# Three rows of score maxima taken in the first stage, output rows prepared in four stages, and other distances in the first stage's chains

## The chip, the cores and the metric

One core of a Trainium2 chip runs the whole kernel. The metric is the device time of one execution in microseconds (us), as the median of several runs. TensorE (PE) does the matmuls, VectorE (DVE), ScalarE (ACT) and GpSimd (POOL) the element work; every transfer here is issued by SyncE (SP). Each engine takes its instructions strictly in the order in which the program holds them.

## What is computed

The reference is one layer of a hybrid encoder block on x of 4096 rows and 1024 columns:

```python
u = rms_norm(h, pre_norm_gain[layer])
proj = jnp.einsum('bsd,de->bse', u, w_in[layer])
fq, fk, fv, fz, ff, rq, rk, rv, rz = jnp.split(proj, split_points, axis=-1)
fox = forgetting_attention(q, k, v, ff + forget_bias)   # 8 heads of 64: causal softmax of
...                                # q.k/8 + c[t] - c[s], c = cumsum(log_sigmoid(f_logit))
fox = fox.reshape(b, s, FOX_WIDTH) * jax.nn.silu(fz)
ret = retention(rq, rk, rv)        # 4 heads of 128: rotation, decayed chunks, group norm
ret = ret.reshape(b, s, RET_WIDTH) * jax.nn.silu(rz)
mixed = jnp.concatenate([fox, ret], axis=-1)
out = jnp.einsum('bse,ed->bsd', mixed, w_out[layer])
h = h + rms_norm(out, post_norm_gain[layer])
```

(The heads' reshapes are left out.) Everything is float32; the kernel gets that accuracy from fp16 pairs (high and low part), with three matmul passes for one product.

## The kernel before

**Stages.** `phase_f0` is the first stage. It computes the input projection of attention heads 0 to 3 (q, k, v, gate z and the forget logits of all 8 heads) for 8 blocks `b` of 512 rows. A block has four units `unit_T` (j = 0 to 3: q, q, k, k) and four units `unit_N` (t = 0 to 3: v and z of 128 rows each). A unit has 8 k-steps of 3 matmuls (6 half-wide ones in `unit_N`). Then `attention()` runs 64 items (one head and one block of 512 queries each). An item of query block qb has 4(qb+1) steps; one step is a pair of score matmuls, two exponentials on ACT (`pf` L1140, `ph` L1141), a subtraction on POOL (`pl` L312) and, six steps later, the product with v. Between attention steps, fillers are issued as long as a credit lasts: the projection of heads 4 to 7 (`fill_f1`), retention in two groups (`fill_r`), and the output projection (`fill_o`). What of `fill_o` is left after the attention runs alone.

**What sets the order.** The program is scheduled by hand. Everything that follows a matmul is a chain, a Python generator in the list `chains`. `tick()` advances every chain by one `yield`; it is called once per k-step of the first stage (`f0_tick`), per attention step and per filler step. So a chain's distance from its source is counted in ticks, and where an instruction stands in its engine's order is fixed when the program is built. A DVE instruction whose input is late holds up all DVE instructions behind it. All PSUM results rotate through 8 banks (`PS()`); a matmul into a bank waits until the bank's last reader is done.

**Weights of the next group.** `scales(1)` reads the 16 tiles of the second projection group (`w_raw`, one transfer `rw` each, issued on SP), takes each one's maximum on DVE (`w_max`, L229) three steps of `SAGE` = 4 ticks after the place of its issue, and then forms the scale. It is started with block 5. `f1.load()`, started with block 6, reads the same tiles again and splits them: ACT writes the high part (L220), DVE the low part (L150). `rw` shares one pool of 12 buffers (`b2`) with the tiles `s2` and `pf`.

**Forget gates.** After each block `forget_block` turns the forget logits into log-sigmoid values (15 small DVE operations, one per tick, and one exponential on ACT), and `VAGE` = 5 ticks later multiplies them on PE with a triangular matrix (`csb`, 128x128, 4 matmuls). These matmuls stand inside the next block's stream, and the same is so for `c_parts`, which splits the cumulated sums into three fp16 parts, one operation per tick, and writes them out.

**Maxima of the score rows.** An item needs, before its first step, a bound on each query's scores. `max_tile()` forms one 128x512 tile of scores on PE, adds a mask on a diagonal tile and reduces it on DVE (L1006). With its last tile an item's `max_row` follows: reduce (L1018), 9 ticks, a transpose on PE (L1024), `mr` on ACT (L1026), two DVE operations, a transfer out (`MR`) and two back into the item's `xq`. `until(("m", n))` lets ticks pass until the last of these is issued. Items 0, 1 and 2 need 4, 8 and 12 tiles. In the last block, items 0 and 1 are done in one burst each, after units t = 0 and t = 1; item 2's tiles go at most two per attention step.

**Evacuation.** `evac_qk` (ACT L401, then DVE L150) empties a `unit_T` bank, `evac_vz` (ACT L425 and L427, then DVE, among it the forget logits at L429) the two banks of a `unit_N`. `rope_evac` empties a q or k bank of retention with ACT (L761) and, `ACTAGE`+1 = 3 ticks later, starts four DVE operations on the copy; the transposes of retention (L818) need the result.

**Output rows.** `prep(n)` prepares 128 rows: a maximum over the row (DVE L1185), small DVE operations, a scaling of the whole tile on ACT (L1188), then two halves of four transposes on PE (L1196) with a copy on ACT and a subtraction on DVE. The first part is issued in one piece. While attention runs, all of `prep` is issued filler step after filler step; in the tail it stands between the matmuls of the row before. `o_final` does the post-norm with a power on POOL.

## Time and profile before

| what | us |
|---|---|
| median of 3 runs | 3123.46 (3123.4 to 3123.75) |
| the profiled execution | 3122.3 |
| its span, first to last instruction | 3120.5 |
| PE busy in the span | 3018.6 (97%) |
| DVE, ACT, POOL busy | 2069.3, 1869.0, 1359.8 |
| first stage, 0 to 428.28 | PE idle in blocks 5 to 7: 3.42, 4.83, 5.39 |
| attention to the first output row, 428.28 to 2677.96 | PE busy 2197.55 of 2249.68 |
| start of the output rows, 2677.96 to 2698.99 | PE busy 11.20 of 21.03 |
| rest, 2698.99 to 3120.5 | PE busy 405.35 of 421.51 |

Every engine but PE has slack over the whole span, so an idle stretch counts where it is PE's. PE's matmuls also run at two clocks: a granted clock (PEclk) of 1.00 or of 0.50, and a stretch at 0.50 holds half the work. The rows behind this are given further down, in numbered groups.

### The profile page before, as it was taken

How to read it: one execution, taken by the hardware profiler on the slowest of the kernel's cores; microseconds unless marked ns; L12 is line 12 of the kernel's file. 1: busy time of each engine (PE TensorE's matmuls, PEld its weight loads, DVE VectorE, ACT ScalarE, POOL GpSimd, SP SyncE). 2: the span in 40 equal slices, each digit the busy share in tenths (PEclk: the TensorE clock that was granted, in tenths of full speed). 3: DMA queues.
4: the chain of work that ended last, by engine and by line, in shares of the span. 5: the costliest groups of instructions: out<-in, count | busy, mean ns of one | idle time of the engine just before them, and what ended most of it. 6: DMA issues, size and time to landing. Idle time of an engine off the chain costs nothing. (4 is left out here: it accounts for less than half of the span.)

```text
span 3120.5 us, 67734 instructions
## 1 busy us (share of the span) xinstructions
PE 3018.6 (97%) x26799; PEld 1789.0 (57%) x26799; DVE 2069.3 (66%) x4372; ACT 1869.0 (60%) x3508; POOL 1359.8 (44%) x1285
## 2 busy tenths in 40 slices
PE   8999979999999999999999999999999999899999
PEld 6666545555555556655555555556566555554554
DVE  6445567445545667786778878776877796645555
ACT  4333335676668666766766776667676766653332
POOL 0000014565555456655655665566455645540000
PEclk9999989999999999999999999999999999999999
DMA  6455744223225231321123214112111321124443
GB/s 182 155 167 146 198 120 106 63 78 98 71 66 131 78 75 49 94 58 43 37 89 82 68 54 125 50 45 74 50 55 46 103 80 37 57 79 139 140 140 118
DMA packets 266174, 284.62 MB, mean 91 GB/s; under 512 B 58976, under 2 KB 212192, under 8 KB 265856
## 3 DMA queue, kind: packets, MB, share of 16 engines
q1 hardware_dynamic: 265856, 280.30, 31.4%
q8 instruction: 210, 3.44, 0.5%
q14 instruction: 108, 0.88, 0.1%
HBM read 194.88 MB, written 88.74 MB: 91 GB/s over the span
## 5 line engine op out<-in xcount | busy, mean ns | idle before, releaser
L312 POOL TENSOR_TENSOR pl<-pf,ph 128x512 f16<-128x512 f32 (+3 forms) x1152 | 1290.4, 1125 | 1095.6 <-ACT ph L1141 829.3
L1140 ACT ACTIVATE pf<-ps,gsc 128x512 f32<-128x512 f32 (+3 forms) x1152 | 757.8, 658 | 668.5 <-PE ps L107 652.8
L1006 DVE TENSOR_REDUCE mrow<-ps 128x1 f32<-128x512 f32 (+3 forms) x1152 | 718.0, 640 | 373.1 <-PE ps L107 362.6
L107 PE MATMUL ps<-wn,xh 128*128 128x512 f16 (+2 forms) x3840 | 853.7, 360 | 4.8 <-DVE qk L150 4.0
L1141 ACT ACTIVATE ph<-ps,gsc 128x512 f16<-128x512 f32 (+3 forms) x1152 | 753.4, 654 | 0.0
L107 PEld LDWEIGHTS <-xh 128*128 128x128 f16 x4608 | 450.6, 98 | 442.6 <-issue 10.5
L107 PE MATMUL ps<-xh,wt 128*128 128x512 f16 x2688 | 666.1, 380 | 1.6 <-DVE mrow L1006 1.0
L107 PEld LDWEIGHTS <-wt 128*128 128x128 f16 x3168 | 308.1, 98 | 349.7 <-issue 18.6
L107 PEld LDWEIGHTS <-ph 128*128 128x128 f16 x8448 | 420.7, 97 | 68.2 <-ACT ph L1141 4.9
L107 PE MATMUL ps<-vt,ph 128*128 128x65 f16 (+1 forms) x8448 | 430.6, 194 | 4.8 <-ACT ph L1141 4.7
L107 PE MATMUL ps<-xq,kc 99*128 99x512 f16 (+3 forms) x1152 | 418.6, 364 | 12.5 <-DMA xq<-MR 9.8
L107 PE MATMUL ps<-vt,pl 128*128 128x65 f16 x4224 | 420.3, 192 | 3.9 <-POOL pl L312 3.9
L107 PE MATMUL ps<-lq,kc 128*128 128x512 f16 (+3 forms) x1152 | 417.5, 363 | 0.0
L107 PE MATMUL ps<-kc,xq 99*128 99x512 f16 (+3 forms) x1152 | 381.3, 362 | 16.5 <-DVE mrow L1006 8.2
L107 PEld LDWEIGHTS <-pl 128*128 128x128 f16 x4224 | 391.5, 99 | 4.9 <-POOL pl L312 4.7
L107 PEld LDWEIGHTS <-kc 128*128 128x128 f16 (+1 forms) x3072 | 280.8, 98 | 196.0 <-issue 21.4
L144 DVE TENSOR_TENSOR s<-s,s 64x512 f32<-64x512 f32 (+1 forms) x256 | 262.0, 1024 | 25.8 <-ACT s L761 13.5
L312 POOL TENSOR_TENSOR sm<-sm,nhalf 128x4 f32<-128x4 f32 (+2 forms) x80 | 62.1, 776 | 350.6 <-DVE sm L147 309.1
L107 PEld LDWEIGHTS <-xq 99*128 99x128 f16 x1152 | 112.0, 98 | 135.8 <-issue 5.7
L107 PE MATMUL ps<-wt,xh 128*128 128x512 f16 x768 | 183.3, 380 | 0.0
L144 DVE TENSOR_TENSOR ps<-ps,maskM 128x128 f32<-128x128 f32 x256 | 74.9, 292 | 122.8 <-PE ps L107 120.8
L144 DVE TENSOR_TENSOR xh<-ps,xh 128x256 f16<-128x256 f32 (+1 forms) x128 | 70.2, 554 | 106.0 <-ACT xh L342 85.3
(120 smaller groups left out, 2520.7 us busy)
## 6 DMA issues: line engine op xcount, KB each, us to landing
xh<-XT SPq DMA_DIRECT2D x176, 256.0 KB
rw<-in_w_in_dram SPq DMA_DIRECT2D x104, 256.0 KB
xt<-in_x_dram SPq DMA_DIRECT2D x36, 512.0 KB
s<-MX SPq DMA_DIRECT2D x32, 512.0 KB
out_dram<-xt SPq DMA_DIRECT2D x31, 512.0 KB
s<-in_x_dram SPq DMA_DIRECT2D x28, 512.0 KB
VD<-s SPq DMA_DIRECT2D x16, 516.0 KB
vt<-VD SPq DMA_DIRECT2D x64, 129.0 KB
```

Source lines behind the costliest of these rows:

```text
L107: nc.tensor.matmul(out=o, lhsT=lhsT, rhs=rhs, start=start, stop=stop, skip_group_check=True)
L144: nc.vector.tensor_tensor(out=o, in0=a, in1=b, op=op)
L312: nc.gpsimd.tensor_tensor(out=o, in0=a, in1=b, op=op)
L1006: nc.vector.tensor_reduce(out=mrow[:, t, c : c + 1], in_=p[:, 0:w], axis=AX.X, op=ALU.max)
L1140: nc.scalar.activation(out=pf[:, q0:512], in_=st[:, q0:512], func=AF.Exp, scale=es)
L1141: nc.scalar.activation(out=ph[:, q0:512], in_=st[:, q0:512], func=AF.Exp, scale=es)
```

## The change

It has seven parts. (1) `ahead_tile()`, called at each k-step of the last block, issues a max tile at every second k-step from the third `unit_T` on, until the tiles of items 0, 1 and 2 (`FIRST` = 3) are out; the two bursts go. (2) `scales(1)` starts with block 4, and takes 8 ticks per weight tile in place of 4. (3) `forget_block` has 3 ticks in place of 2 at its start and 10 in place of 5 ahead of its matmuls; `c_parts` has 3 (`CAGE`) in place of 1 between its operations. (4) In `evac_vz` the DVE operation of the forget logits moves behind the tick. (5) `rope_evac` has 2 ticks in place of 3. (6) `prep` is cut into four stages (maximum, scaling, two transposes); with attention alive, `PSTEP` = 3 attention steps lie behind each, and in the tail a fourth place, (0, 4), is added; a factor D moves into `ep`. (7) `o_final` loses one addition on POOL and one operation on DVE per row (32 rows), and waits for POOL by ticks of its own.

```diff
--- before.py
+++ after.py
@@ -47,6 +47,9 @@
 CREDIT = 6000.0
 OAGE = 4
 PWAIT = 2
+CAGE = 3
+FIRST = 3
+PSTEP = 3
 ACTAGE = 2
 POOLAGE = 4
 ACCAGE = 3
@@ -292,7 +295,7 @@
             for i in range(len(todo) + 2):
                 if i < len(todo):
                     raws.append(w_raw(g, *todo[i]))
-                for _ in range(SAGE):
+                for _ in range(2 * SAGE if g == 1 else SAGE):
                     yield 1
                 if i >= 2:
                     w_max(mk, i - 2, raws[i - 2])
@@ -425,10 +428,10 @@
         nc.scalar.activation(out=vst[:, :, t, 0:64], in_=pvh, func=AF.Copy, scale=f)
         th = SB("z1", [128, 256])
         nc.scalar.activation(out=th, in_=pz, func=AF.Tanh, scale=izh(g, 1))
+        for _ in range(ACTAGE if g else 1):
+            yield 1
         if pf_ is not None:
             stt(ff[:, t, :], pf_, iz(g, 1), fbb, ALU.mult, ALU.add)
-        for _ in range(ACTAGE if g else 1):
-            yield 1
         stt(vst[:, :, t, 65:129], pvh, f, vst[:, :, t, 0:64], ALU.mult, ALU.subtract)
         stt(zs[:, :, t % 2, :], th.rearrange("p (h d) -> p h d", h=4), 1.0, pz.rearrange("p (h d) -> p h d", h=4), ALU.add, ALU.mult)
         for _ in range(3):
@@ -448,8 +451,8 @@
         y = SB("sm", [128, n])
         q = SB("sm", [128, n])
         y2 = SB("sm", [128, n])
-        yield 1
-        yield 1
+        for _ in range(3):
+            yield 1
         stt(a, f, -1.0, f, ALU.mult, ALU.min)
         yield 1
         nc.scalar.activation(out=e, in_=a, func=AF.Exp)
@@ -472,7 +475,7 @@
         yield 1
         lf = SB("sm", [128, 4, FH])
         stt(lf.rearrange("p t h -> p (t h)"), q, -2.0, a, ALU.mult, ALU.add)
-        for _ in range(VAGE):
+        for _ in range(2 * VAGE):
             yield 1
         p = PS()
         for t in range(4):
@@ -500,15 +503,20 @@
     def c_parts(c, v, h1, h23, g, n):
 
         ts(v, c, gsc[g][0][0:n, KT + 7 : KT + 8], None, ALU.mult, ALU.bypass)
-        yield 1
+        for _ in range(CAGE):
+            yield 1
         nc.scalar.activation(out=h1, in_=v, func=AF.Copy, scale=1.0 / (TOP * CP))
-        yield 1
+        for _ in range(CAGE):
+            yield 1
         stt(v, h1, -TOP * CP, v, ALU.mult, ALU.add)
-        yield 1
+        for _ in range(CAGE):
+            yield 1
         nc.scalar.activation(out=h23[:, 0], in_=v, func=AF.Copy, scale=1.0 / MID)
-        yield 1
+        for _ in range(CAGE):
+            yield 1
         stt(v, h23[:, 0], -MID, v, ALU.mult, ALU.add)
-        yield 1
+        for _ in range(CAGE):
+            yield 1
         nc.scalar.activation(out=h23[:, 1], in_=v, func=AF.Copy, scale=1.0 / LOW)
         for _ in range(3):
             yield 1
@@ -637,7 +645,15 @@
                         xs, t0, k = todo.pop(0)
                         spawn(a_k(b + 1, xs, t0, k, nX))
 
-            if b == max(0, NB - 3):
+            ahead = [0]
+
+            def ahead_tile():
+
+                ahead[0] += 1
+                if not more and NB > 4 and ahead[0] > 2 * KT and ahead[0] % 2 and mlist[mdone[0]][0] < FIRST:
+                    max_tile()
+
+            if b == max(0, NB - 4):
                 spawn(scales(1))
             if b == NB - 2:
                 spawn(f1.load())
@@ -654,6 +670,7 @@
                     p = PS()
                     for k in unit_T(W[0], X, j * 128, p):
                         f0_tick()
+                        ahead_tile()
                         if not more and j == 3:
                             f1.release("wt", k)
                     spawn(evac_qk(p, 0, b, j))
@@ -664,12 +681,10 @@
                 last = not more and t == 3
                 for k in unit_N(W[1], X, t, ((0, 256), (256, 520)), [pa[:, 0:256], pb[:, 0:264]]):
                     f0_tick()
+                    ahead_tile()
                     if last:
                         f1.release("wn", k)
                 spawn(evac_vz(pa[:, 0:256], pb[:, 0:256], 0, b, t, vst, zst, pb[:, 256:264], ff))
-                if not more and t < 2 and NB > 4:
-                    for _ in max_tiles(t):
-                        f0_tick()
             assert not todo
             if not more:
                 f1.X = X
@@ -759,7 +774,7 @@
 
     def rope_evac(p, rp, o, key):
         nc.scalar.activation(out=o, in_=p, func=AF.Copy, scale=iz(key[1], 0))
-        for _ in range(ACTAGE + 1):
+        for _ in range(2):
             yield 1
         t2 = SB("s2", [128, 512])
         tt(t2[0:64], o[64:128], rp[64:128, 1, :], ALU.mult)
@@ -1185,10 +1200,11 @@
             nc.vector.tensor_reduce(out=am[:, 0:1], in_=rows, axis=AX.X, op=ALU.max, apply_absolute_value=True)
             ts(am[:, 0:1], am[:, 0:1], 1e-6, 1.0 / 16384.0, ALU.max, ALU.mult)
             nc.vector.reciprocal(out=am[:, 1:2], in_=am[:, 0:1])
+            ep = SB("sm", [128, 2])
+            ts(ep[:, 0:1], am[:, 1:2], math.sqrt(NORM_EPS * D), gsc[4][0][:, KT + 2 : KT + 3], ALU.mult, ALU.mult)
+            tt(ep[:, 1:2], ep[:, 0:1], ep[:, 0:1], ALU.mult)
+            yield 0
             nc.scalar.activation(out=rows, in_=rows, func=AF.Copy, scale=am[:, 1:2])
-            ep = SB("sm", [128, 2])
-            ts(ep[:, 0:1], am[:, 1:2], math.sqrt(NORM_EPS), gsc[4][0][:, KT + 2 : KT + 3], ALU.mult, ALU.mult)
-            tt(ep[:, 1:2], ep[:, 0:1], ep[:, 0:1], ALU.mult)
             yield 0
             for half in range(2):
                 p = PS()
@@ -1207,13 +1223,20 @@
             yield 1
 
         def o_final(y, ss, xr, r0_, ep):
-            yield 1
-            ptt(ss[:, 2:3], ss[:, 0:1], ss[:, 1:2], ALU.add)
-            r = yield from rstd_of(ss[:, 2:3], 1, 1.0 / D, ep[:, 1:2])
+            v, r, a = ss[:, 2:3], ss[:, 3:4], SB("sm", [128, 1])
+            for _ in range(2 if attn_alive[0] else 1):
+                yield 1
+            stt(v, ss[:, 0:1], ss[:, 1:2], ep[:, 1:2], ALU.add, ALU.add)
+            ptt(r, v, nhalf[:, 0:1], ALU.pow)
+            for _ in range(5 if attn_alive[0] else 2):
+                yield 1
+            stt(a, v, r, r, ALU.mult, ALU.mult)
+            ts(a, a, -0.5 * math.sqrt(D), 1.5 * math.sqrt(D), ALU.mult, ALU.add)
+            tt(r, r, a, ALU.mult)
             parts = 2 if r0_ + 128 == S else 1
             for i in range(parts):
                 cs = slice(i * D // parts, (i + 1) * D // parts)
-                stt(y[:, cs], y[:, cs], r[:, 0:1], xr[:, cs], ALU.mult, ALU.add)
+                stt(y[:, cs], y[:, cs], r, xr[:, cs], ALU.mult, ALU.add)
                 yield 1
                 dma(out2[r0_ : r0_ + 128, cs], y[:, cs])
 
@@ -1226,7 +1249,11 @@
                 start = gstep[0] + OAGE
                 while attn_alive[0] and gstep[0] < start:
                     yield -1
-                yield from prep(n)
+                for c in prep(n):
+                    yield c
+                    start = gstep[0] + PSTEP
+                    while attn_alive[0] and gstep[0] < start:
+                        yield -1
                 if attn_alive[0]:
                     for _ in range(PWAIT):
                         yield WAIT
@@ -1250,6 +1277,8 @@
                     yield WAIT if k is None else 3 * COST_MM + pump(k)
                     if (hf, k) == (0, 1) and n + 1 in mxs:
                         nxt = prep(n + 1)
+                        yield next(nxt)
+                    if nxt is not None and (hf, k) == (0, 4):
                         yield next(nxt)
                     if nxt is not None and hf == 1 and k in (1, 4):
                         yield next(nxt)
```

The order of instructions moves at three places of interest (names are tile, a running number and an id; lines are those of each kernel, L153 of after is L150 of before).

DVE in the last block of the first stage, before. `wn_707` is the low part of the weight tile whose raw tile is `rw_697`; `s2_709<-ps_708` are the first readers of the forget matmuls' bank, and `qk_714<-ps_704` empties the bank of unit j = 2:

```order
L150 SCALAR_TENSOR_TENSOR qk_703_4579<-ps_699_4535,gsc00_8_150,qk_703_4579 128x512
L150 SCALAR_TENSOR_TENSOR wn_702_4575<-rw_667_4430,gsc11_11_153,wn_702_4575 128x512
L150 SCALAR_TENSOR_TENSOR wn_707_4600<-rw_697_4512,gsc11_11_153,wn_707_4600 128x512
L147 TENSOR_SCALAR s2_709_4616<-ps_708_4611,s2_605_3998 8x128
L147 TENSOR_SCALAR s2_709_4616<-ps_708_4611,s2_709_4616 8x128 x3
L147 TENSOR_SCALAR s2_712_4624<-s2_709_4616,gsc00_8_150 4x512
L150 SCALAR_TENSOR_TENSOR s2_712_4624<-s2_710_4622,s2_712_4624 4x512
L150 SCALAR_TENSOR_TENSOR qk_714_4636<-ps_704_4581,gsc00_8_150,qk_714_4636 128x512
```

The same place after. `ps_711`, `ps_712`, `ps_718` and `ps_719` are max tiles, `s2_721<-ps_720` reads the forget matmuls' bank:

```order
L147 TENSOR_TENSOR ps_711_4616<-ps_711_4616,maskM_4_146 128x128
L1021 TENSOR_REDUCE mrow_705_4586<-ps_711_4616 128x1
L153 SCALAR_TENSOR_TENSOR wn_710_4609<-rw_697_4511,gsc11_11_153,wn_710_4609 128x512
L147 TENSOR_TENSOR ps_712_4627<-ps_712_4627,maskM_4_146 128x128
L1021 TENSOR_REDUCE mrow_705_4586<-ps_712_4627 128x1
L1033 TENSOR_REDUCE sm_713_4631<-mrow_705_4586 128x4
L150 TENSOR_SCALAR sm_713_4631<-sm_713_4631,gsc00_8_150 128x4
L153 SCALAR_TENSOR_TENSOR qk_715_4639<-ps_704_4579,gsc00_8_150,qk_715_4639 128x512
L1021 TENSOR_REDUCE mrow_717_4646<-ps_718_4647 128x1
L1021 TENSOR_REDUCE mrow_717_4646<-ps_719_4656 128x1
L150 TENSOR_SCALAR s2_721_4667<-ps_720_4662,s2_609_4032 8x128
```

Max tiles stand ahead of and behind the weight tile now, and the readers of the forget matmuls' bank stand behind `qk_715`, where they stood ahead of `qk_714`.

DVE, item 2's max row, before: after the attention has begun, beside `qk_817<-ps_774`, an evacuation of the second projection group, which runs as filler; `mrow_786` is item 2's row:

```order
L150 SCALAR_TENSOR_TENSOR qk_817_5193<-ps_774_5019,gsc10_10_152,qk_817_5193 128x512
L144 TENSOR_TENSOR ps_831_5237<-ps_831_5237,maskM_4_146 128x128
L1006 TENSOR_REDUCE mrow_786_5059<-ps_831_5237 128x1
L144 TENSOR_TENSOR ps_832_5241<-ps_832_5241,maskM_4_146 128x128
L1006 TENSOR_REDUCE mrow_786_5059<-ps_832_5241 128x1
L1018 TENSOR_REDUCE sm_833_5245<-mrow_786_5059 128x4
L147 TENSOR_SCALAR sm_833_5245<-sm_833_5245,gsc00_8_150 128x4
```

After: still in the first stage, ahead of `evac_vz` of its last unit (`sm_675`, `s4_729`, `s2_763`); `mrow_747` is item 2's row:

```order
L147 TENSOR_TENSOR ps_769_5000<-ps_769_5000,maskM_4_146 128x128
L1021 TENSOR_REDUCE mrow_747_4812<-ps_769_5000 128x1
L147 TENSOR_TENSOR ps_770_5016<-ps_770_5016,maskM_4_146 128x128
L1021 TENSOR_REDUCE mrow_747_4812<-ps_770_5016 128x1
L1033 TENSOR_REDUCE sm_771_5020<-mrow_747_4812 128x4
L150 TENSOR_SCALAR sm_771_5020<-sm_771_5020,gsc00_8_150 128x4
L153 SCALAR_TENSOR_TENSOR sm_675_4444<-ps_766_4956,gsc01_9_151,fbb_6_148 128x8
L153 SCALAR_TENSOR_TENSOR s4_729_4702<-ps_765_4955,s4_729_4702 128x4x64
L153 SCALAR_TENSOR_TENSOR s2_763_4951<-z1_772_5030,ps_766_4956 128x4x64
```

Item 2's row has moved from the attention's third item into the last unit of the first stage.

ACT at the first output row, before. `s4_8372` is the row tile that is scaled (L1188), `xh` are the copies of the two transposed halves:

```order
L1140 ACTIVATE pf_8390_41814<-ps_8388_41810,gsc10_10_152 128x512
L1141 ACTIVATE ph_8391_41815<-ps_8388_41810,gsc10_10_152 128x512
L1188 ACTIVATE s4_8372_41718<-s4_8372_41718,sm_8394_41824 128x1024
L342 CAST xh_8397_41837<-ps_8396_41832 128x512
L342 CAST xh_8399_41845<-ps_8398_41840 128x512
L1140 ACTIVATE pf_8400_41850<-ps_8389_41811,gsc10_10_152 128x512
L1141 ACTIVATE ph_8401_41851<-ps_8389_41811,gsc10_10_152 128x512
```

After (L1207 is the scaling, L345 the copy):

```order
L1041 ACTIVATE mr_8424_41994<-ps_8423_41992 4x128
L1207 ACTIVATE s4_8387_41803<-s4_8387_41803,sm_8408_41909 128x1024
L1155 ACTIVATE pf_8426_42002<-ps_8419_41983,gsc10_10_152 128x512
L1156 ACTIVATE ph_8427_42003<-ps_8419_41983,gsc10_10_152 128x512
L1155 ACTIVATE pf_8431_42013<-ps_8429_42009,gsc10_10_152 128x512
L1156 ACTIVATE ph_8432_42014<-ps_8429_42009,gsc10_10_152 128x512
L1155 ACTIVATE pf_8434_42021<-ps_8430_42010,gsc10_10_152 128x512
L1156 ACTIVATE ph_8435_42022<-ps_8430_42010,gsc10_10_152 128x512
L345 CAST xh_8438_42034<-ps_8437_42029 128x512
```

The scaling has the exponentials of further attention steps ahead of it, and more of them between it and the first copy.

## Rows read from the trace of the kernel before

**Rows 1.** Page, part 1: busy us, share of the span, instructions.

```profile
PE 3018.6 (97%) x26799; PEld 1789.0 (57%) x26799; DVE 2069.3 (66%) x4372; ACT 1869.0 (60%) x3508; POOL 1359.8 (44%) x1285
```

**Rows 2.** Windows: length, busy PE, PEld, DVE, ACT, POOL, PEclk, DMA share, GB/s.

```profile
371.93:428.28 56.35, 50.96 (x312) 32.17 (x310) 27.23 (x75) 12.39 (x25) 0.00 (x0) 0.91 0.51 137
428.28:2677.96 2249.68, 2197.55 (x21406) 1287.70 (x21403) 1590.93 (x3147) 1531.36 (x2820) 1261.10 (x1137) 1.00 0.26 72
2677.96:2698.99 21.03, 11.20 (x134) 7.42 (x132) 16.49 (x27) 11.81 (x20) 8.96 (x7) 0.76 0.45 131
```

**Rows 3.** Windows of the eight stretches at the lower clock, same columns; last their sum.

```profile
334.91:341.73 6.82, 4.90 (x16) 2.09 (x17) 6.21 (x16) 3.47 (x7) 0.81 (x2) 0.50 0.93 233
403.17:410.00 6.83, 5.99 (x28) 4.21 (x28) 6.59 (x17) 2.57 (x6) 0.00 (x0) 0.50 0.41 101
...
454.38:468.02 13.64, 5.68 (x14) 2.05 (x15) 7.17 (x15) 4.56 (x11) 1.84 (x3) 0.50 0.45 110
2686.69:2696.92 10.23, 3.06 (x13) 2.29 (x14) 7.23 (x15) 2.63 (x5) 2.67 (x2) 0.50 0.17 51
2741.31:2748.12 6.81, 5.28 (x36) 3.91 (x37) 2.36 (x4) 4.49 (x8) 5.19 (x5) 0.50 0.01 2
...
sum 54.55, PE 35.12 PEld 19.26 DVE 36.12 ACT 19.76 POOL 13.51; mean PE 4.39 PEld 2.41 DVE 4.51 ACT 2.47 POOL 1.69
```

**Rows 4.** Timeline, PE and DVE, forget matmuls in blocks 5, 6: start, us, [idle before].

```profile
283.21 1.44 PE L107 MATMUL ps<-csb,sm 128*8 128x128 f32 x8 [3.42 <-DVE sm L150]
...
336.83 1.45 PE L107 MATMUL ps<-csb,sm 128*8 128x128 f32 x6 [4.83 <-DVE sm L150]
...
335.14 0.69 DVE L229 TENSOR_REDUCE mk<-rw 128x1 f32<-128x512 f32 x1 [6.39 <-DMA rw<-in_w_in_dram]
```

**Rows 5.** Timeline of the last block: PE, ACT, DVE, SP's queue.

```profile
371.93 14.41 PE L107 MATMUL ps<-xh,wt 128*128 128x512 f16 x66
...
404.01 8.28 PE L107 MATMUL ps<-wn,xh 128*128 128x264 f16 x47 [3.07 <-DVE qk L150]
...
395.14 0.72 ACT L220 ACTIVATE wn<-rw,gsc 128x512 f16<-128x512 f32 x1 [11.96 <-DMA rw<-in_w_in_dram]
...
395.89 0.75 DVE L150 SCALAR_TENSOR_TENSOR wn<-rw,gsc,wn 128x512 f16<-128x512 f32 x1 [11.27 <-ACT wn L220]
...
374.15 4.27 SPq L110 DMA_DIRECT2D xq<-QX  x4
...
391.75 0.43 SPq L110 DMA_DIRECT2D rw<-in_w_in_dram  x1
```

**Rows 6.** Timeline, item 2's max row: DVE's reduce, PE's first step.

```profile
446.05 0.17 DVE L1018 TENSOR_REDUCE sm<-mrow 128x4 f32<-128x12 f32 x1
...
462.34 0.58 PE L107 MATMUL ps<-xq,kc 99*128 99x512 f16 x1 [9.85 <-DMA xq<-MR]
```

**Rows 7.** Timeline, PE and ACT at the first output row.

```profile
2693.86 1.97 PE L1196 MATMUL ps<-csb,s 128*128 128x128 f32 x8 [9.84 <-ACT s L1188]
...
2692.66 1.15 ACT L1188 ACTIVATE s<-s,sm 128x1024 f32<-128x1024 f32 x1 [5.79 <-DVE sm L1187]
```

**Rows 8.** Timeline, ACT and PE at the second output row.

```profile
2738.29 1.15 ACT L1188 ACTIVATE s<-s,sm 128x1024 f32<-128x1024 f32 x1 [5.62 <-DVE sm L1187]
...
2740.64 0.23 PE L107 MATMUL ps<-vt,ph 128*128 128x65 f16 x2 [3.52 <-ACT ph L1141]
```

**Rows 9.** Waits: engine and line, releaser: total us, times, longest.

```profile
DVE sm L150 <- ACT z L427: 65.3, 30, 4.1
...
DVE s L144 <- ACT s L761: 13.5, 5, 7.2
...
PE ps L818 <- DVE s L144: 11.1, 13, 2.9
```

**Rows 10.** Page, part 5: groups: busy us, mean ns | idle before.

```profile
L1140 ACT ACTIVATE pf<-ps,gsc 128x512 f32<-128x512 f32 (+3 forms) x1152 | 757.8, 658 | 668.5 <-PE ps L107 652.8
L1006 DVE TENSOR_REDUCE mrow<-ps 128x1 f32<-128x512 f32 (+3 forms) x1152 | 718.0, 640 | 373.1 <-PE ps L107 362.6
```

## The prediction

> **What bounds the kernel now.** I read the busy line first: PE works 3018.6 of 3120.5 us [rows 1], so what can be won without less work for PE is the 101.9 us in which it idles, and what it loses at the lower clock. The windows show where that lies [rows 2]: the whole attention stretch idles 52 us in 2250, in crumbs, while the last block of the first stage idles 5.4 of 56 and the start of the output rows 9.8 of 21. Then I listed PE's idle stretches over 2 us, and behind each looked for the stretch in which the granted clock is 0.50. There are eight of these; PE is busy 35.12 us in them [rows 3], and since the same work takes half as long at 1.00, they cost 17.6 us besides the idle time. Each follows a wait of PE of more than 2 us; three that are not shown hold 3.4 us of busy time each. Last, I followed each large wait back to what came late. Five causes hold nearly all of it, and each is touched by the change; the other losses are crumbs. My sum is made against the profiled execution, 3122.3 us (span 3120.5); the median is 1.2 us above it.
>
> **A, forget matmuls of blocks 5 and 6.** PE waits 3.42 and 4.83 us for DVE's forget values [rows 4]. DVE stands still at a weight maximum whose raw tile has not landed (6.39 us before block 6's, 4.86 before block 5's [rows 4]); the forget operations are queued behind it. With the slow clock behind, 4.90/2 = 2.45 [rows 3] and 3.4/2 = 1.7, this costs 3.42 + 4.83 + 2.45 + 1.7 = 12.4. The change doubles the distance from 12 to 24 ticks. A tick here is three matmuls, 14.41/66 x 3 = 0.655 us [rows 5], so 24 are 15.7 us. Before, the tile landed some 12 x 0.655 + 6.39 = 14.3 us after its place: now in time. The forget matmuls also stand 6 ticks (3.9 us) later, and nothing waits for these but the next cumulated sum. The 16 transfers start a block earlier, among the same other ones but less crowded. **Gain 12**, bounds 6 (half of the distance eaten up by later landing) and 12.4.
>
> **B, the last block.** It idles 56.35 - 50.96 = 5.4 us [rows 2], and two slow stretches cost 5.99/2 [rows 3] and 3.4/2: 10.0 in all. The cause: SP first issues the attention's loads, from 374.15 on, and reaches the raw weight tile only at 391.75; ACT takes it at 395.14 after 11.96 us of waiting, DVE at 395.89 after 11.27, and the evacuations behind it release PE's banks late [rows 5]. The change doesn't move this transfer ahead of those loads. But it puts max tiles and the evacuation of unit j = 2 between it and the first reader of the forget bank on DVE (the first pair of order rows). That bank comes eight allocations after the bank of that unit, so the forget matmuls wait for it. PE gets there after 48 + 24 matmuls, five tiles, 12 matmuls and two tiles: 84 x 0.218 + 1.0 = 19.3 us, at 391.2. DVE is done with `qk_715` at 395.89 + 0.75 + a masked tile (0.3 + 0.64 [rows 10]) + 0.4 + 0.7 = 398.6. So PE waits 7.3 us there, in place of the 3.07 and the smaller waits of now, with a slow stretch behind (5.7/2 = 3 [rows 3], as after the 9.85 wait). The 24 tiles also put 24 x 0.64 = 15.4 us on a DVE that is 27.23 busy of 56 there [rows 2]; behind the jam I estimate 2 us more of waits in unit t = 1, 1.3 in t = 3 and 1 at the attention's start, each below the 3.07 that PE waited there for DVE [rows 5]. Cost after: 7.3 + 3 + 2 + 1.3 + 1 = 14.6, **-5**. Bounds +10 (no jam) and -9 (the waits behind it double).
>
> **C, item 2's max row.** Its reduce is at 446.05 and PE starts the item at 462.34, after 9.85 us of waiting [rows 6], since the 12 tiles are formed in the attention's first steps and the chain from reduce to `xq` takes 16.3 us. The slow stretch around it adds 5.68/2 = 2.84 [rows 3]. After the change the reduce stands in the last unit of the first stage (the second pair of order rows), and 12 attention steps stand before the item. These took from 428.28 [rows 2] to 452.5 (462.34 - 9.85), 24 us, more than 16.3. The row's transfers keep their place in SP's order relative to the chain. **Gain 12.7**, bounds 9 (a slower chain, 20 us, with DVE's backlog) and 12.7.
>
> **D, the first output row.** PE waits 9.84 us for the scaling on ACT [rows 7], and 3.06/2 = 1.5 for the clock [rows 3]; ACT waits 5.79 for DVE's reciprocal [rows 7], 7 us behind PE by then. In four stages this wait is spread over attention steps: three between stages (third pair of order rows). But until the rows are prepared there is no filler: some 19 steps in a row without one, where before there were about 8. Such steps are bound by ACT, 2 x 0.66 [rows 10] = 1.3 us each, or 25 us, where PE has work for about 19 (1.0 a step: two score matmuls and a max tile at 0.218, and twelve short ones); so PE idles about 6 in small pieces. **Gain 11.3 - 6 = 5**, bounds 0 and 11.
>
> **E, ACT held by the scaling near the attention's end.** At the second output row ACT waits 5.62 us for DVE, and PE 3.52 for the exponentials behind it [rows 8], then 0.99 and 0.97 for POOL, with 5.28/2 = 2.64 for the clock [rows 3]. A second such place follows 32 us later (PE 1.19 + 1.00, clock 1.7). Together 12.0. With the maximum three steps ahead of the scaling, DVE has 4 us more and the wait is 1.6 or none; the no-filler crumbs of D come back here. **Gain 8**, bounds 3 and 12.
>
> **F, retention's rotation.** The transposes wait 11.1 us for it in 13 cases [rows 9]. One tick less puts the four DVE operations ahead of at most one max tile (0.64 [rows 10]) more, in perhaps half of 32 heads and blocks: 32 x 0.5 x 0.64 = 10, of which half where PE waited: **gain 5**, bounds 0 and 11.
>
> **At nothing:** the later forget logits (DVE waits 65.3 us for ACT there [rows 9], and no PE wait names it; if the cover were gone, bound 0 to 1 in the last block's t units); `CAGE` (stored parts are read a block later at the earliest, for block 7 in the attention's last items of a head); `o_final` (32 small operations on POOL and DVE, off PE's path but for the last row: 0.2, bounds 0 and 0.6).
>
> **Sum:** 12 - 5 + 12.7 + 5 + 8 + 5 = 37.7; 3122.3 - 37.7 = 3084.6, and 1.2 on top for the median: **3086**.
>
> **The rivals.**
> R1, no jam in the last block: the raw tile lands before DVE needs it, so B gives its 10 back instead of costing 5. 3086 - 15 = 3071. For it: its place in SP's order is early in program ticks. Against: 27 issues from 374.15 to 391.75 stand ahead on SP [rows 5], and none has moved. The Trainium skill, "DMA: Bandwidth & Descriptors", section "Issuing engines are not separate DMA queues", calls the time to initiate a DMA usually small relative to the DMA itself; by that the tile would be early and R1 right. The trace disagrees: 17.6 us go into issuing, 3.4 lie from issue to ACT's start. Chance 0.14.
> R2, the waits come back under new names: the weight tiles of blocks 4 to 6 land later still (A 0), the spread stages starve PE as long as the one wait did (D 0), ACT is held again (E 3). 3086 + 12 + 5 + 5 = 3108. For it: DVE and ACT are in order, and the distance is counted in ticks, not in time. Chance 0.15.
> R3, the slow clock stays through the last block: after its jam further waits of 1 to 2 us follow each other, so most of its remaining 35 us run at 0.50. In the trace the block has two slow stretches, with one between them at 1.00 (mean PEclk 0.91 [rows 2]). 35/2 = 17: 3103. The Trainium skill, "TensorE: Matmul & The Clock Gate", section "A second HAM failure mode: psum-queue depth-cycling", speaks against this change: cycling through banks with frequent small idles makes the clock go up and down. In this trace the slow stretches follow waits of over 2 us, which bears it out only in part. Chance 0.08.
> R4, item 2's row is late all the same (DVE's backlog): C 0. 3086 + 12.7 = 3099. Chance 0.07. R2 and R4 at once: 3120, no difference. Chance 0.03.
> R5, slower: with one tick less, `rope_evac`'s first DVE operation reaches its place before ACT's copy, in all 64 cases instead of 5 (13.5 us now [rows 9]), and everything behind it on DVE waits, the max tiles' banks too. At one exponential that ACT is behind, 0.66 us [rows 10], it costs 64 x 0.66 = 42 and F's 5: 3086 + 5 + 42 = 3133. It reaches zero from 0.51 us per case (32.7/64), if DVE's wait goes to PE in full; DVE is 71% busy in the attention (1590.93 of 2249.68 [rows 2]), which speaks against. Chance 0.05.
>
> **How the numbers follow.** The forecast has 0.48. A measurement of this kernel tells about 0.2%, 6 us, from no change. Faster by more than that: all cases but the last two, 0.92; same 0.03; slower 0.05. The range has to reach R1 (3071), R3, R4 and R2 (3108) and the terms' bounds (A to F all at their best: 12.4 + 10 + 12.7 + 11 + 12 + 11 = 69, 3054; at their worst 6 - 9 + 9 + 0 + 3 + 0 = 9, 3114; not all at once): 3061 to 3110.
>
> **What the profile after would show.** A: no PE wait at the forget matmuls of blocks 5 and 6, and PEclk 1.00 there. B: one PE wait of 7 us for `qk` or `sm` at the forget matmuls of the last block, about 391, and a longer block than 56 us; R1 if it is shorter. C: PE's first step of item 2 without `xq<-MR`. D: no wait over 2 us around the first output row, but many under 1 for `ph` and `pl`. E: ACT's waits for L1187 gone. F: L818's row under 7 us; R5 if the `s <- s L761` wait has over 40 us. I am wrong in A if a weight tile still ends DVE's wait, and in the whole if the attention's 2250 us stretch grows by more than 10.

## The result, and the profile after

The changed kernel takes 3084.86 us (3082.9 to 3086.8), the kernel before 3123.43 us on the same chip; the ratio is 0.9876, 95% interval 0.9865 to 0.9888. The forecast was 3086, in a range of 3061 to 3110. So the total is right. Its terms are not: two of them miss by more than 11 us, in opposite directions, and that is what the experiments are about. (Further down, three executions of the kernel before and one of p_rope1 took 4365 to 8254 us, in a slow state of the chip; medians include them, ratios and traces do not.)

The busy line of the profiled execution (span 3085.0, answering [rows 1]):

```profile
PE 3011.5 (98%) x26799; PEld 1789.2 (58%) x26799; DVE 2063.7 (67%) x4340; ACT 1874.4 (61%) x3508; POOL 1350.5 (44%) x1253
```

PE has the same 26799 instructions and idles 73.5 us in place of 101.9. The stretches of the first stage and of the attention, as windows with the columns of [rows 2] (blocks 5 and 6, the last block, the attention from its first to its 1104th step, the rest):

```profile
257.53:308.00 50.47, 50.47 (x363) 35.67 (x362) 28.80 (x92) 18.23 (x45) 1.56 (x3) 1.00 0.59 178
308.00:359.90 51.90, 51.90 (x376) 36.91 (x374) 34.02 (x98) 23.24 (x52) 2.20 (x4) 1.00 0.79 217
359.90:412.25 52.35, 48.68 (x325) 31.01 (x323) 34.34 (x91) 12.32 (x25) 0.00 (x0) 1.00 0.57 151
...
412.53:2661.95 2249.42, 2203.85 (x21456) 1294.34 (x21455) 1586.01 (x3138) 1541.32 (x2829) 1259.48 (x1140) 0.99 0.26 72
2661.95:3085.00 423.05, 408.51 (x2540) 215.96 (x2538) 238.37 (x518) 176.62 (x331) 76.49 (x84) 0.99 0.38 121
```

Blocks 5 and 6 have no idle time on PE at all, and the last block is 4.0 us shorter, at full clock throughout. But the attention's 1104 steps, which have lost the 9.85 us wait and the slow stretch around it [rows 3, 6], 12.7 us together, take 2249.4 us where the same steps took 2254.9 before:

```profile
428.61:2683.53 2254.92, 2202.79 (x21468) 1290.82 (x21467) 1596.04 (x3155) 1535.99 (x2829) 1263.41 (x1140) 1.00 0.26 72
```

More than half of what they gained was spent again inside.

To see where, I worked out PE's loss for every run: for each PE instruction the time to the next one's start, less the median of that time over all runs for instructions of the same kind, summed over a stretch. It contains idle time and what the lower clock costs. The stretches are the first stage from block 1 to the last block, the last block, the attention's steps 0 to 48, 48 to 1104 of 1152, and from there to the end (the first 79 us, with 15 to 19 in every run, are left out):

| PE's loss, us | blocks 1 to 6 | last block | steps 0 to 48 | steps 48 to 1104 | to the end |
|---|---|---|---|---|---|
| before | 13.4 | 11.2 | 14.9 | 59.7 | 25.6 |
| after | 1.3 | 4.9 | 2.9 | 68.5 | 11.7 |
| difference | -12.1 | -6.3 | -12.0 | +8.8 | -13.9 |
| forecast | A -12 | B +5 | C -12.7 | F -5 | D, E -13 |

Of the 59.7 us, 3.0 fall into slow-clock stretches; of the 68.5, 12.2. So the idle time of steps 48 to 1104 is the same (56.7 and 56.3), and the loss is the clock: two slow stretches there before, seven after. The waits that grew, as rows of waits by engine and line (total us, times, longest), of after:

```profile
PE ps L110 <- DVE mrow L1021: 21.8, 21, 2.9
PE ps L833 <- DVE s L147: 8.4, 6, 3.2
PE ps L110 <- DVE state L153: 8.3, 10, 1.5
```

Waits for the reduces of max tiles were 14.5 us before, at most 1.6 each; now some reach 2.9. The row of before:

```profile
PE ps L107 <- DVE mrow L1006: 14.5, 23, 1.6
```

The wait for the rotation (L833 is L818 of before) fell from 11.1 [rows 9] to 8.4, in fewer and longer pieces.

### The profile page after: what moved, and what is told of

It is laid out like the page before. It is cut to its first block, busy times and chain, and to the rows that moved or that the text cites. A ratio compares the mean times of both kernels' runs of the same rounds, so it can differ in the third digit from the quotient of the medians.

```text
span 3085.0 us, 67707 instructions
## 1 busy us (share of the span) xinstructions
PE 3011.5 (98%) x26799; PEld 1789.2 (58%) x26799; DVE 2063.7 (67%) x4340; ACT 1874.4 (61%) x3508; POOL 1350.5 (44%) x1253
## 4 chain that ended last, share of the span: by engine, by line
PE 83%; DVE 11%; issue 2%; ACT 1%; POOL 1%; DMA 1%; SPq 1%; POOLq 0%; DVEq 0%; ACTq 0%
PE ps L110 80%; DVE mrow L1021 3%; DVE s L147 2%; POOL pl L315 1%; PE ps L1212 1%; PE ps L356 1%; DVE s L150 1%; SPq L113 1%; ACT pf L1155 1%; DVE sm L150 1%; ACT ph L1156 1%; DVE s L153 1%; DMA rw<-in_w_in_dram 0%; DVE wn L153 0%; DVE state L153 0%
## 5 line engine op out<-in xcount | busy, mean ns | idle before, releaser
L110 PEld LDWEIGHTS <-xh 128*128 128x128 f16 x4608 | 448.2, 98 | 444.5 <-issue 12.6
L315 POOL TENSOR_TENSOR sm<-sm,nhalf 128x4 f32<-128x4 f32 (+2 forms) x80 | 61.8, 772 | 646.1 <-DVE sm L153 324.9
L147 DVE TENSOR_TENSOR s<-s,s 64x512 f32<-64x512 f32 (+1 forms) x256 | 254.2, 993 | 21.0 <-ACT s L776 11.1
```

The source lines that it names most:

```text
L110: nc.tensor.matmul(out=o, lhsT=lhsT, rhs=rhs, start=start, stop=stop, skip_group_check=True)
L147: nc.vector.tensor_tensor(out=o, in0=a, in1=b, op=op)
L315: nc.gpsimd.tensor_tensor(out=o, in0=a, in1=b, op=op)
```

## The experiments

The kernels ran in three groups; each group shares one chip and the runs of the kernel before on it. The same loss by stretch tells what each edit does where:

| PE's loss, us | blocks 1 to 6 | last block | steps 0 to 48 | steps 48 to 1104 | to the end | ratio to before (95%) |
|---|---|---|---|---|---|---|
| b_rope2 | 15.3 | 8.0 | 14.8 | 54.4 | 25.1 | 0.9968 (0.9957 to 0.998) |
| b_tiles | 14.2 | 8.2 | 4.1 | 71.2 | 17.7 | 0.9953 (0.9938 to 0.9968) |
| b_prep | 14.1 | 11.3 | 14.5 | 61.8 | 17.4 | 0.9965 (0.9952 to 0.9978) |
| b_weights | 1.4 | 8.1 | 13.8 | 61.6 | 26.0 | 0.9946 (0.9932 to 0.9961) |
| a_rope3 | 1.4 | 6.8 | 2.9 | 74.6 | 12.3 | 0.9888 (0.9873 to 0.9903) |
| b_tiles_phase | 14.3 | 8.3 | 2.4 | 60.9 | 25.6 | 0.9951 (0.9934 to 0.9967) |
| before_shift | 16.7 | 10.5 | 17.4 | 72.3 | 17.7 | 1.0015 (1.0005 to 1.0024) |
| after_phase | 1.4 | 5.4 | 0.6 | 58.2 | 14.9 | 0.9836 (0.9821 to 0.985) |
| after_again | 1.3 | 6.1 | 2.9 | 66.7 | 11.7 | 0.9875 (0.9858 to 0.9892) |
| p_raw | 1.3 | 0.9 | 6.9 | 58.8 | 14.2 | 0.9854 (0.9834 to 0.9873) |
| p_rope1 | 1.3 | 5.2 | 0.6 | 63.1 | 15.8 | 0.9873 (0.9854 to 0.9892) |
| p_pstep0 | 1.3 | 6.4 | 0.6 | 58.6 | 13.6 | 0.9844 (0.9827 to 0.9861) |

Two runs of the changed kernel (after, after_again) differ by up to 1.8 in a stretch, and stretches that an edit does not reach by up to 3.3 (blocks 1 to 6 of before and before_shift, 13.4 and 16.7; the last block of before and b_rope2, 11.2 and 8.0); smaller differences are not read. The row of before is one execution of 3122.3 us. On the chips of the three groups before takes 3127.12, 3125.38 and 3125.15 us, so a gain in time against the chip's own before is up to 5.5 us larger than what the rows tell (b_prep: 11.2 and 5.7). Each row is one trace.

### Each part alone

**The rotation.** The first suspect for the attention's 8.8 us was the part that touches it. Taken back in the changed kernel (a_rope3), and made alone in the kernel before (b_rope2):

```diff
 def rope_evac(p, rp, o, key):
...
-        for _ in range(2):                 # a_rope3; b_rope2 is the reverse
+        for _ in range(ACTAGE + 1):
             yield 1
```

> The changed kernel with the three ticks of before in rope_evac. In the attention up to its 1104th step the changed kernel lost about 9 us against before, nearly all of it in more stretches at the lower clock. Theory 1 (the earlier rotation puts four DVE operations ahead of max tiles, whose banks PE then waits for, over 2 us at a time): this kernel loses those 9 us no more and comes to about 3076 us, with the low-clock stretches of the attention back from eight to two or three. Theory 2 (the tiles of item 2 done early shift the whole plan of max tiles, and that is where the 9 us come from): about 3085 us, or 3090 if the prediction's gain of 5 us from the rotation is real.

> The kernel before with only the rotation's three ticks cut to two. Theory 1 (the rotation's earlier place costs 9 us in the attention): about 3132 us. The prediction's term F: about 3118 us, with the wait of the transposes at L818 under 7 us. Theory 2 (the plan of max tiles): 3123 us, no difference.

Measured: a_rope3 3091.73 (before 3127.12 on this chip), b_rope2 3117.09, a gain of 10.0. The suspect falls: the shorter distance gains in both kernels, 59.7 to 54.4 in steps 48 to 1104 of the kernel before, 74.6 to 68.5 in the changed one (whose ratios alone, 0.9888 and 0.9876, have intervals that overlap). In b_rope2 the wait row of the transposes drops from 11.1 us to this, while the DVE's wait for ACT's copy doubles from 13.5:

```profile
DVE s L144 <- ACT s L761: 26.0, 10, 7.4
...
PE ps L818 <- DVE s L144: 3.0, 4, 1.3
```

**The max tiles alone** (`ahead_tile` in, the two bursts out; nothing else):

```diff
+                        ahead_tile()              # in both loops over k-steps
...
-                if not more and t < 2 and NB > 4:
-                    for _ in max_tiles(t):
-                        f0_tick()
```

> The kernel before with only the 24 max tiles of items 0, 1 and 2 spread over the last block of the first stage. Both theories: PE no longer waits for item 2's row (12.7 us). Theory 1: the rest of the attention is as before, and the last block's own 11 us stay or fall to 5: 3105 to 3111 us. Theory 2: the attention up to its 1104th step loses 9 us besides: 3114 to 3120 us. By the prediction's count of banks (the bank of unit j = 2 is the one that the forget matmuls wait for) the last block is longer than before by 5 us: 3116 us.

Measured: 3112.97, a gain of 14.2. The total lies between what the two theories gave, and the stretches decide: item 2's wait is gone (14.9 to 4.1), the last block is no longer, and steps 48 to 1104 lose 11.5, as theory 2 said; the end gives back 7.9, which neither had. But one part of theory 2 is wrong: counted from the programs, the number of max tiles at each step from the 48th on is the same as before. What differs is the filler. The 12 tiles no longer count 216 each toward the credit of the attention's first steps, so the filler stands 5 k-steps further back at step 48, and 2 to 5 up to step 1056. That gave theory 3, below.

**The output rows alone** (parts 6 and 7 of the change: four stages, `PSTEP` = 3, the shorter `o_final`):

> The kernel before with only the output rows' preparation in four stages and the new o_final. If terms D and E of the prediction are what they were put at (5 and 8 us), about 3110 us, with no wait of PE for L1188's counterpart; if the gain of the end came from elsewhere (less filler left for the tail, an earlier arrival), 3118 us or more. Theory 2 in another form (the spread stages move the max tiles near the attention's end) would show as a loss ahead of the 1104th step, where this kernel should be as before.

Measured: 3115.92, a gain of 11.2 (13 was expected). The end's loss goes from 25.6 to 17.4, the wait for the scaling is gone, and steps 48 to 1104 lose 2.1, within what two runs differ by. Parts 6 and 7 were not run apart.

**The weight reading and the forget gates alone** (parts 2 and 3; the forget logits stay where they were):

```diff
-                for _ in range(SAGE):
+                for _ in range(2 * SAGE if g == 1 else SAGE):
...
-            if b == max(0, NB - 3):
+            if b == max(0, NB - 4):
                 spawn(scales(1))
```

> The kernel before with the weight reading one block earlier at twice the distance, and the longer distances in the forget block and in the parts of the sums; the forget logits' operation stays where it was. Term A of the prediction: no PE wait at the forget matmuls of blocks 5 and 6, 12 us less before the last block, none elsewhere: 3111 us where before takes 3123. If the transfers land later in their new place, 6 us less: 3117 us. The last block holds its jam: as long as before within 3 us.

Measured: 3108.73 against 3125.38, a gain of 16.7. In the trace 12.0 of it lies in blocks 1 to 6, as term A said; the 3.1 in the last block is not read, since b_rope2 has as much there without an edit. The DVE's waits for raw tiles, before and in b_weights (waits rows, L230 is the same line):

```profile
DVE mk L229 <- DMA rw<-in_w_in_dram: 13.1, 5, 6.4
...
DVE mk L230 <- DMA rw<-in_w_in_dram: 2.0, 4, 0.7
```

That these waits go is the doing of part 2. Part 3, which puts the forget matmuls 6 ticks (3.9 us) later, was not run without it, so how much it would have hidden alone is not known. Part 4 was not run alone at all.

### Where the filler stands

Theory 3: it is the filler's place against the attention's steps, a few k-steps, that decides which DVE work meets in one step. It can be moved without moving anything else: the 216 of cost can be counted without the tiles, or taken off with them.

```diff
                 gstep[0] += 1
+                if 3 <= gstep[0] < 15:
+                    cost += 216            # b_tiles_phase, after_phase; before_shift: cost -= 216
                 for _ in range(max_rate(gstep[0])):
```

With it, the programs of b_tiles_phase and before hold the same number of filler matmuls at all steps compared (every 48th), after_phase up to the 1104th, and before_shift is where b_tiles was.

> The kernel before with the 24 tiles in the first stage, and 216 of cost counted in each of the attention's steps 3 to 14 for the 12 tiles that are no longer formed there. So the filler stands at every attention step where it stood before; in the kernel with the tiles alone it stood 2 to 5 k-steps further back. Theory 3 (where the filler stands against the attention's steps sets what meets on DVE, and the shift of a few k-steps cost the kernel with the tiles alone some 11 us between the 48th and the 1104th step): that loss is gone, 3127 - 25 = 3102 us by the clock of the chip of the earlier runs. Rival (the loss comes from the earlier tiles themselves, as from buffers that are held): 3113 us, as without the cost.

> The changed kernel with the same cost counted in steps 3 to 14, so that the filler stands where it stood before at least up to the 1104th step. Theory 3: the stretch from the 48th to the 1104th step loses 9 to 15 us less than in the changed kernel, 0.9876 of before becomes 0.984, some 3073 us where before takes 3123. Rival: no difference to the changed kernel, 0.9876 of before.

> The kernel before with 216 less counted in each of the attention's steps 3 to 14: the filler stands 2 to 5 k-steps further back, as in the kernel with the tiles alone, and nothing else is changed. Theory 3: some 11 us slower than before between the 48th and the 1104th step, about 3134 us where before takes 3123. Rival: within 3 us of before.

Measured: in steps 48 to 1104 the filler's place is the cause in all three. Moving the filler alone costs 12.6 (before_shift, 59.7 to 72.3), or 10.7 against b_weights (61.6), whose filler was not moved, on the same chip; putting it back regains 10.3 with the tiles (71.2 to 60.9) and 8.5 to 10.3 in the changed kernel (66.7 and 68.5 to 58.2). Seven slow stretches stand in that part of before_shift, three in b_tiles_phase, four in after_phase, two in before. The waits of PE for max tiles follow; these rows are of before_shift, b_tiles, b_tiles_phase and after_phase, where before had 14.5, 23, 1.6:

```profile
PE ps L107 <- DVE mrow L1006: 23.2, 24, 2.9
```

```profile
PE ps L108 <- DVE mrow L1014: 23.9, 24, 2.9
```

```profile
PE ps L108 <- DVE mrow L1014: 14.3, 22, 1.6
```

```profile
PE ps L110 <- DVE mrow L1021: 16.0, 24, 1.6
```

Which DVE operations meet in which step was not followed up; shown are the effect of the filler's place and the longer waits. Only one shift was tried, so nothing says that further back is worse in general.

What I had not expected is the end. With the filler further back (level at step 1104, 2 to 5 k-steps back again from step 1110 on) the end loses 17.7 in place of 25.6, both in b_tiles and in before_shift, where no output row is prepared otherwise. So b_tiles_phase, which undoes the shift, wins 10 us in the middle and gives 8 back at the end: 3109.87, a ratio of 0.9951 where b_tiles had 0.9953. The expected 3102 was wrong for that reason, and so was the 3134 of before_shift: it takes 3130.37 against 3125.38, ratio 1.0015. In after_phase the four stages hold the end at 14.9 without the shift (11.7 with it, in after), and most of the middle's gain is kept: 3074.17 against 3125.38 before, ratio 0.9836. It beats both kernels.

### What is left, on after_phase

after_again is the changed kernel on the chip of the three others; these are after_phase with one number changed each: `RAWAGE * 3` in place of `* 2` for the second group (p_raw), one tick in place of two in `rope_evac` (p_rope1), `PSTEP = 0` (p_pstep0).

> The changed kernel once more, on the chip of the three kernels that follow, which are built on it with the cost of the 12 tiles counted (after_phase). Expected: 0.9876 of before, as at first, and some 11 us above what after_phase had against its before (0.9836).

> The changed kernel with the tiles' cost counted in steps 3 to 14, and with 24 in place of 16 ticks between the issue of a raw weight tile of the second group and its use. In the changed kernel's last block of the first stage DVE stood 7.9 us at a weight tile, with the evacuation of unit j = 2 behind it, and PE then waited 1.26 and 0.84 us and some shorter times, 4 us in all over what the block has at best. Theory (the late raw tile is still what these waits come from, only on other banks than the prediction named): they go, 2 to 4 us less than after_phase in this block, 0.9825 of before. Rival (the waits come from 24 tiles on DVE, wherever the weight tile stands): the block as long as in after_phase.

> The changed kernel with the tiles' cost counted, and rope_evac with one tick in place of two. If the order on DVE alone decides (term F goes on): 0 to 3 us less than after_phase, since 2.9 us of waiting at L833 are left. By rival R5 of the prediction: the first DVE operation now comes before ACT's copy is done in most of 64 cases, DVE's wait for ACT at the copy rises from some 12 us to over 40, and the kernel is 10 to 40 us slower than after_phase.

> The changed kernel with the tiles' cost counted, and with PSTEP = 0: the four stages of an output row's preparation follow each other filler step after filler step while attention runs. By terms D and E of the prediction the attention steps between the stages are what takes the wait away: PE waits again some 8 to 10 us at the first output row and 2 to 4 us behind ACT's scaling, 8 to 13 us more than after_phase. Rival (the cut into four stages, or the later place in the program, is enough): within 4 us of after_phase.

after_again: 3085.52, ratio 0.9875, as at first.

p_raw: 3078.84, 0.9854; the expected 0.9825 is missed, and the interval reaches after_phase's. The theory is right for its block and wrong for the kernel. The last block's loss goes from 5.4 to 0.9, so its waits did come from the late weight tile. But the tiles of the next group are now split later, and at the attention's start PE meets a new wait with a slow stretch behind it, 6.3 us more in steps 0 to 48 (timeline of PE, p_raw):

```profile
430.17 0.26 PE L110 MATMUL ps<-kc,xq 99*128 99x128 f16 x1 [3.26 <-DVE qk L153]
```

p_rope1: 3085.13, 0.9873, slower than after_phase by about 11 by the ratios. It looks like rival R5 in small: the DVE's wait for ACT's copy has risen from 26.0 us in 10 cases (after_phase) to 30.4 in 15, not to 40 in 64, and PE waits longer for max tiles and for retention's state (16.0 and 7.1 in after_phase):

```profile
PE ps L110 <- DVE mrow L1020: 20.0, 29, 2.3
PE ps L110 <- DVE state L153: 11.9, 14, 2.1
...
DVE s L147 <- ACT s L776: 30.4, 15, 7.4
```

The trace shows 4.9 us more loss in steps 48 to 1104 and 0.9 at the end. The rest of the 11 is not in the two traces, whose spans are 3081.5 and 3075.0; they are of the fastest execution of p_rope1 and the slowest of after_phase.

p_pstep0: 3074.41, 0.9844, the same as after_phase. The rival holds. PE's long wait at the first output row is back, as expected, and ACT's behind DVE (p_pstep0, PE and ACT):

```profile
2662.72 1.97 PE L1214 MATMUL ps<-csb,s 128*128 128x128 f32 x8 [8.75 <-ACT s L1209]
...
2661.52 1.15 ACT L1209 ACTIVATE s<-s,sm 128x1024 f32<-128x1024 f32 x1 [4.71 <-DVE sm L1204]
```

And yet the end loses 13.6, not more than after_phase with its 14.9. The attention steps between the stages take away one wait of 8.75 us and cost as much elsewhere. From step 1104 on after_phase has these waits, where p_pstep0 has none for `pl` and 1.4 us for `xt`:

```profile
PE ps L110 <- POOL pl L315: 5.3, 7, 1.0
PE ps L110 <- DVE xt L147: 3.2, 1, 3.2
```

## Why the prediction was right, and where not

**A held**: forecast 12, measured 12.1 in the changed kernel and 12.0 in b_weights. No tile ends a DVE wait in these blocks for more than 0.8 us.

**B was wrong, and the step that failed is "that bank comes eight allocations after the bank of that unit, so the forget matmuls wait for it".** All that the step rests on came true. SP reached the raw tile at the same distance from the block's start (19.5 us, before 19.8), ACT started on it at 22.7, DVE at 23.5, and the forget matmuls stood at 19.8 (forecast 19.3, with seven max tiles ahead of them where there are six). Timeline of the last block after, PE, then DVE, ACT and SP:

```profile
379.68 1.04 PE L110 MATMUL ps<-csb,sm 128*8 128x128 f32 x8
...
385.12 0.27 PE L110 MATMUL ps<-wn,xh 128*128 128x256 f16 x1 [1.26 <-DVE mrow L1021]
386.23 0.72 PE L110 MATMUL ps<-wn,xh 128*128 128x264 f16 x5 [0.84 <-DVE qk L153]
...
383.38 0.75 DVE L153 SCALAR_TENSOR_TENSOR wn<-rw,gsc,wn 128x512 f16<-128x512 f32 x1 [7.90 <-ACT wn L223]
...
385.43 0.74 DVE L153 SCALAR_TENSOR_TENSOR qk<-ps,gsc,qk 128x512 f16<-128x512 f32 x1
...
382.63 0.72 ACT L223 ACTIVATE wn<-rw,gsc 128x512 f16<-128x512 f32 x1 [11.48 <-DMA rw<-in_w_in_dram]
...
379.38 0.44 SPq L113 DMA_DIRECT2D rw<-in_w_in_dram  x1
```

But the forget matmuls ran without idle time; those that waited came 5.4 and 6.6 us later, for a max tile's reduce and then for `qk`, 2.1 us together, with no slow stretch behind. So the banks are not handed out in a strict circle of eight: the bank of unit j = 2 was needed next by the first `unit_N`, not by the forget matmuls. I took the circle from the pool's size and never looked for a row of before that shows it. The program as built from the changed kernel shows the rule. The forget matmuls' tile `ps_720` lies in bank 7, which the max tile `ps_706` held, and the bank 4 of `ps_704` goes to `ps_731` of the first `unit_N`. A max tile is reduced early, so its bank is free early. Over the whole program after, the next tile takes the bank whose last use stands earliest in 2990 of 3124 cases, and the bank of eight tiles ago in 266. Measured -6.3 against +5: nearest to R1's +10 for this block, but by another way (the tile was as late as ever). Up to 3.3 of the 6.3 can be the difference between two runs; after_again, after_phase and a_rope3, at 5.4 to 6.8, also lose less there than any kernel built on before (8.0 to 11.3).

**C held:** 12.0 against 12.7.

**F held for what it spoke of and missed what decided the stretch.** The rotation's shorter distance gains 5.3 in steps 48 to 1104 of the kernel before and 6.1 in the changed one; forecast 5. Its sign, the transposes' wait under 7 us, is met in b_rope2 (3.0) and after_phase (2.9) and missed in after (8.4), where the filler stands further back. The stretch lost 8.8 all the same, because the filler moved by 2 to 5 k-steps, which costs 8.5 to 12.6 us. The prediction has no step for that. It counted where item 2's tiles went and what they freed, not that their cost feeds the credit that paces the filler for the rest of the attention. That is the failed step: the change was costed by the instructions it moves, and one thing it moves is a number. The sign of being wrong that was given, the attention longer by more than 10, could not show it: item 2's 12.7 us went out of the same stretch, which came out 5.5 shorter.

**D and E:** forecast 13, measured 13.9, with the parts wrongly shared. D's picture was right: the 9.84 us wait is gone, and in its place PE waits in small pieces (PE and ACT after, around the first output row), with 5.05/2 = 2.5 us for a slow stretch from 2671.8 on (its window last):

```profile
2665.40 0.20 PE L110 MATMUL ps<-vt,pl 128*128 128x65 f16 x1 [1.05 <-POOL pl L315]
...
2670.85 0.20 PE L110 MATMUL ps<-vt,pl 128*128 128x65 f16 x1 [1.02 <-POOL pl L315]
...
2673.55 0.38 PE L1039 MATMUL ps<-csb,sm 128*4 128x128 f32 x1 [1.78 <-DVE sm L150]
...
2675.03 1.15 ACT L1207 ACTIVATE s<-s,sm 128x1024 f32<-128x1024 f32 x1 [0.81 <-DVE sm L1202]
...
2671.80:2678.60 6.80, 5.05 (x38) 3.15 (x39) 3.84 (x10) 5.10 (x9) 3.96 (x5) 0.50 0.00 2
```

p_pstep0 shows that D as a whole is worth about nothing, where I gave it 5. The rest falls where E had put it, at the waits behind the second output row, but not for E's reason, that the maximum stands three steps ahead of the scaling. These waits of PE (3.52, then 1.19 us) are gone in after, and just so in p_pstep0, which has no steps in between, and in before_shift and b_tiles, where `prep` is as before. ACT's wait for DVE at the scaling, which was to be gone, falls from 29.4 us in 9 cases (before, from 2683.5 to 2860) to 10.4 in 5 (after, from 2661.9 to 2830). How the end's 13.9 us are shared between the cut into stages and the shift stays open: b_prep (-8.2), after_phase (-10.7) and before_shift (-7.9) each have one of them, and after has 13.9 with both.

**The sum.** 37.7 was forecast and 35.5 is what PE's loss fell by. B gave 11.3 more than forecast, the attention 13.8 less. That the two cancel is luck, and the sum is right by it. B's gain of 6.3 lies inside its bounds (+10 to -9), the attention's loss of 8.8 outside F's (0 to 11), and no rival named either mechanism. Had B been right, the time would have been 3096; had the filler been foreseen and B not, the forecast would have been 3100.

R2, R3, R4 and R5 did not come. R3's slow clock did, but in the attention. The prediction's list of eight slow stretches has none there, though before has two in steps 48 to 1104 (from 1570.5 and 1963.1 on), and two of its eight, from 416.83 and 2775.44 on, have only waits of at most 0.58 and 1.19 us in the 6 us ahead of them, none of over 2. R1's 27 issues on SP are 28 in its rows. The Trainium skill ("TensorE: Matmul & The Clock Gate", section "A second HAM failure mode: psum-queue depth-cycling") says that cycling through PSUM banks can make TensorE idle often enough for its clock to swing. In steps 48 to 1104 this trace agrees only in part: at equal idle time, 56.7 and 56.3 us, the slow stretches cost 3.0 and 12.2, but six of the seven in after have a single wait of 1.94 to 3.17 us ahead of them or in them, and only that from 1722.85 on has several shorter ones (0.64, 0.86, 0.83 and 1.47). In the last block, for which I had cited it, it does not: PEclk is 1.00 there.

## What to carry to other kernels

Where a budget or a credit paces one stream of work against another, an edit that changes the counted cost moves the whole stream: compare how far the paced work stands at the same step of the other, before and after, and give that its own term. Hold it fixed to measure the edit. And add up the parts of a change by stretch and from traces: the four runs with one part or two alone gain 52 us in time, each against before on its own chip, where the whole gains 38.6; but PE's loss falls by 36.2 in the four together and by 35.5 in the whole. So the traces show no more of the parts acting on each other than two runs differ by; where the times' other 16 us lie is not known. And when a wait is forecast on a rotating buffer, find a row in the trace that shows which use waits for which; a pool's size does not tell it.

## What the runs showed of the hardware

The length of one wait does not tell whether the slow clock follows. After two waits of over 2.3 us the clock stayed at 1.00, and after two of 1.9 to 2.0 it fell to 0.50 (PE's timeline after; the last row is of before, where the clock stayed at 1.00 behind a wait of 2.51):

```profile
1918.26 0.59 PE L110 MATMUL ps<-kc,xq 99*128 99x512 f16 x2 [2.32 <-DVE mrow L1021]
...
1945.66 0.63 PE L833 MATMUL ps<-csb,s 128*128 128x128 f32 x4 [2.36 <-DVE s L147]
...
2309.12 0.81 PE L110 MATMUL ps<-xh,wt 128*128 128x512 f16 x3 [1.94 <-DVE mrow L1021]
...
2520.29 0.38 PE L110 MATMUL ps<-xq,kc 99*128 99x512 f16 x1 [1.97 <-DVE mrow L1021]
...
974.12 0.23 PE L107 MATMUL ps<-kc,xq 99*128 99x128 f16 x1 [2.51 <-DMA kc<-KX]
```

The granted clock behind the first, the second, the third and the fourth of these (windows of after, columns of [rows 2]), and behind the wait of before:

```profile
1915.60:1922.00 6.40, 4.08 (x64) 2.74 (x62) 6.23 (x15) 1.66 (x4) 1.84 (x2) 1.00 0.24 82
1942.90:1949.00 6.10, 3.74 (x27) 1.93 (x26) 4.52 (x7) 3.08 (x6) 2.05 (x2) 1.00 0.01 3
```

```profile
2309.90:2313.30 3.40, 3.40 (x52) 2.79 (x49) 1.32 (x3) 0.00 (x0) 0.00 (x0) 0.51 0.22 82
2521.60:2525.00 3.40, 3.40 (x36) 2.30 (x35) 3.37 (x8) 0.65 (x2) 1.15 (x1) 0.50 0.56 168
...
974.10:980.00 5.90, 5.88 (x70) 3.60 (x71) 3.72 (x7) 3.17 (x6) 2.56 (x3) 1.00 0.66 182
```

So my prediction's reading, that slow stretches go with waits of over 2 us, is too simple, and the trace of before already showed it. What decides besides the wait's length, such as what PE did around it, was not tried apart.
